# Pieces of one mixer stream placed behind another stream's products in a hybrid trunk kernel

## The chip, the cores and the metric

The kernel runs on one core of a Trainium2 chip. The metric is the time of one execution on the device in microseconds (us). The engines that the text names are TensorE (PE: matrix products and transposes by a product with the identity; PEld is its weight load), VectorE (DVE), ScalarE (ACT), GpSimd (POOL) and SyncE (SP), whose queue issues most of the DMA transfers. Each engine executes its own instructions in program order and waits for the others by semaphores.

## The reference

One layer of a hybrid trunk is applied to a prompt of 16 + 2048 frames and to a sample of 64 frames. An input projection feeds three parallel mixers, whose outputs go through an output projection; a SwiGLU FFN follows. All inputs and outputs are float32.

```python
def _mixer(h, ...):
    proj = h @ w_in                              # 1024 -> 5384
    z, xbc, dt_raw, rw_in, hg_in = _split(proj)  # SSD, RWKV-7, HGRN2 columns
    # Mamba-2 SSD, 8 heads, state 64 x 128
    h = h * exp(cum[-1]) + (xg * exp(cum[-1] - cum)) @ Bm
    y = (L * (Cm @ Bm)) @ xg + (Cm @ h) * exp(cum)
    # RWKV-7, 8 heads, state 64 x 64
    S = S * w + (S @ a) b + v k ;  o = S @ r
    # HGRN2, 4 heads, state 128 x 128
    A = sum(dec * q * k) ;  o = A @ v + (q * exp(cum)) @ S
    S = S * exp(cum[-1]) + (k * exp(cum[-1] - cum)) @ v
    return concat(y_ssd, y_rw, y_hg) @ w_out
x = x + _mixer(rmsnorm(x)) ;  x = x + swiglu(rmsnorm(x)) ;  return rmsnorm(x)
```

Each mixer carries a state from one group of frames to the next, so the tiles of a mixer have to be worked through one after the other.

## The kernel before, in words

**Tiles and stages.** The frames lie in 17 tiles (0 to 16) of up to 128 frames; a chunk has two or three tiles, and there are six chunks (0 to 5), two to a projection block. Weights and activations are split in a high and a low part, and a product is made of three matmuls (high by high, high by low, low by high). The stages are

1. the projection of three blocks (`projection()`), which writes its results to DRAM, where the mixers fetch them tile by tile;
2. the early FFNs for tiles 0 to 8 (`early()`): output projection (`out`), SwiGLU column groups (`ffn`), and the last of its second projection (`rest`). The last of these FFNs stops after 18 column groups (`SWITCH = 18`);
3. `drain(ALLY(range(NT)))` (L1423): every mixer tile has to be done here. Then the `ya` tiles of the late stage are loaded from what the mixers stored (L1434, 24 DMAs on SP), and the last early FFN goes on (`ffn(SWITCH, NFF)`, `rest()`);
4. the late stage for tiles 9 to 16, whose first products have the names `g<-w,op`; `op` is made from `ya` (L1416, L1417).

The matmuls of stages 1, 2 and 4 are called products here; their PSUM banks are named `g` (late also `d`).

**The mixers as streams.** The mixers are Python generators, and a piece is what one yields. RWKV (`rw_mixer`, banks `c` and `po`) is one stream, `rw`. HGRN (`hg_mixer`, L758) and SSD (`ss_mixer`, L886) are woven into one other, `hs` (`hs_mixer`, L979): a step of it runs one piece of HGRN and one of SSD, some 13 steps to a tile. Both write the PSUM bank `h`, of which there is one (L514). HGRN's input tile `hin` also exists once (L761): its last part K is written by L882 and stored by L883 (GpSimd's queue), and the load for the next tile, on SP, waits for that. SSD loads `sin` and `dec` in the same way, one buffer each. `dt`, `cu` and `ex` (L464 and following) are made once for each chunk, in four buffers, and are last used by SSD.

**What sets the order.** Products are generators too, which yield their length in units of 2360 columns (`COL`). `flow` adds it to a clock `now`, and steps every stream whose due time `t` the clock has reached. A step sets t to max(t, now − 1) + d · scale, where d is what the piece yields; for `hs` that is 6.0 × 1.03 = 6.18 units a step. `drain` steps the streams without the clock, until the tiles asked for are done. From the instructions in the order in which they are written down like this, a scheduler sets the final order on each engine by its own model of the times, so that an instruction can move against its neighbours.

The core of it, before:

```python
        def step(self):
            d = next(self.gen, None)
            if d is None:
                self.live = False
            else:
                self.t = max(self.t, now[0] - 1.0) + d * self.scale
    ...
    def flow(gen):
        for cost in gen:
            now[0] += cost
            for s in list(streams):
                while s.live and s.t <= now[0]:
                    s.step()
```

Of the kernel before, what the change touches and what calls it, by code (L numbers as in the profile page):

```python
# [19 lines left out]
P = 128  # L20
# [19 lines left out]
GLO = 3  # L40
URB = 6
RWX, HSX, HSD = 1.08, 1.03, 6.0
COL = 1 / 2360
AHEAD = 4
KOUT = [8, 9, 10, 11, 0, 1, 2, 3, 4, 5, 6, 7]
# [33 lines left out]
def body(tc, A, O, blocks=None, supers=None, dbg=None):  # L79
    nc = tc.nc  # L80
    V, S, G, T = nc.vector, nc.scalar, nc.gpsimd, nc.tensor
# [26 lines left out]

    def mm(out, lhsT, rhs, start, stop, more=False):

        return T.matmul(out, lhsT, rhs, start=start, stop=stop, skip_group_check=more)  # L111

    def in_turn(ins):

# [4 lines left out]
    flat = lambda ap: ap.rearrange("p a b -> p (a b)")  # L119
# [36 lines left out]
    ident = cload("ident", [P, P], p=cst)  # L156
# [91 lines left out]
    def transposed(h, k4, n, hi, lo, col, bank):  # L248

        pt = by(bank(), P)  # L250
        for k in range(4):
            T.transpose(pt[:, k, :n], h[:n, k * P:(k + 1) * P], ident[:n, :n])
        ho, lw = (x[:, 4 * k4:4 * k4 + 4, col:col + n] for x in (hi, lo))
        S.activation(ho, pt[:, :, :n], AF.Copy)
        V.tensor_tensor(lw, pt[:, :, :n], ho.bitcast(F32), SUB)
# [46 lines left out]
    class Chunk:  # L302
        def __init__(self, ci):
            self.ci, self.tiles = ci, CHUNKS[ci]
            self.lens = [LEN[t] for t in self.tiles]
            self.N = sum(self.lens)
            self.nt = len(self.tiles)
            self.offs = [sum(self.lens[:i]) for i in range(self.nt)]
            self.first = self.tiles[0] == 0
# [120 lines left out]
        def dt(self, ps):  # L430

            N, nt = self.N, self.nt
            q0 = 32 * (self.ci % 2)
            st, idq = dst[q0:q0 + 16], ident[q0:q0 + 16, q0:q0 + 16]
            S.activation(st[:, :N], ps[:16, :N], AF.Copy)
            yield
            pt = by(gbank()[:, :48], 16)
            for j in range(nt):
                n, o = self.lens[j], self.offs[j]
                T.transpose(pt[:n, j, :], st[:, o:o + n], idq)  # L440
            sm = lambda tag: mk(gp, [P, 3, 8], tag=tag, bufs=1)[:, :nt]
            dx, ax, u, u2, pl = sm("dx"), sm("ax"), sm("du"), sm("du2"), sm("pl")
            bias = _bc(cb[:, 0:8], 1, nt)
            if self.first:
                G.memset(dx, 0.0)
                V.tensor_tensor(dx[:80, 0, :], pt[:80, 0, 0:8], cb[:80, 0:8], ADD)
                V.tensor_tensor(dx[:, 1:, :], pt[:, 1:nt, 0:8], bias[:, 1:], ADD)
                V.tensor_tensor(dx[:80, 0, :], pt[:80, 0, 8:16], dx[:80, 0, :], ADD)
                V.tensor_tensor(dx[:, 1:, :], pt[:, 1:nt, 8:16], dx[:, 1:, :], ADD)
            else:  # L450
                V.tensor_tensor(dx, pt[:, :nt, 0:8], bias, ADD)
                V.tensor_tensor(dx, pt[:, :nt, 8:16], dx, ADD)
            V.scalar_tensor_tensor(ax, dx, -1.0, dx, MUL, MAX)
            S.activation(ax, ax, AF.Exp, scale=-1.0)
            V.tensor_scalar(u, ax, 2.0, None, ADD)
            V.reciprocal(u, u)
            V.tensor_tensor(u, u, ax, MUL)
            V.tensor_tensor(u2, u, u, MUL)
            V.tensor_scalar(pl, u2, 1.0 / 15.0, None, MUL)
            for k in (13, 11, 9, 7, 5, 3):  # L460
                V.scalar_tensor_tensor(pl, pl, 1.0 / k, u2, ADD, MUL)
            V.scalar_tensor_tensor(pl, pl, 1.0, u, ADD, MUL)
            V.tensor_scalar(dx, dx, 0.0, None, MAX)
            res = mk(dtp, [P, 2, 3, 8], tag="dt", bufs=4)  # L464
            V.scalar_tensor_tensor(res[:, 0, :nt], pl, 2.0, dx, MUL, ADD)
            if self.first:
                V.tensor_scalar(res[:, 0, 0], res[:, 0, 0], c("vmask"), None, MUL)
            la = res[:, 1]
            V.tensor_tensor(la[:, :nt], res[:, 0, :nt], _bc(nea, 1, nt), MUL)

            j0 = 1 if self.first else 0
            yield
            p1 = gbank()[:, 0:72].rearrange("p (a j h) -> p a j h", a=3, h=8)
            mm(flat(p1[:, 0, j0:nt]), triu, flat(la[:, j0:nt]), True, True)
            mm(flat(p1[:, 1, j0:nt]), ones, flat(la[:, j0:nt]), True, True)
            if self.first:
                mm(p1[:, 0, 0], triu0, la[:, 0], True, True)
                mm(p1[:, 1, 0], blk1, la[:, 0], True, True)
                mm(p1[:, 2, 0], ones[0:64, :], la[0:64, 0], True, True)
            cu = mk(dtp, [P, 3, 8], tag="cu", bufs=4)  # L480
            ex = mk(dtp, [P, 3, 3, 8], tag="ex", bufs=4)
            V.tensor_copy(cu[:, :nt], p1[:, 0, :nt])
            V.tensor_copy(ex[:, 0, :nt], p1[:, 0, :nt])
            V.tensor_tensor(ex[:, 1, :nt], p1[:, 1, :nt], cu[:, :nt], SUB)
            V.tensor_copy(ex[:, 2, j0:nt], p1[:, 1, j0:nt])
            if self.first:
                V.tensor_copy(ex[:, 2, 0], p1[:, 2, 0])
            S.activation(ex[:, :, :nt], ex[:, :, :nt], AF.Exp)
            if self.first:
                V.tensor_scalar(ex[:, 0, 0], ex[:, 0, 0], c("smask"), None, MUL)  # L490
            yield
            pt = gbank()
            for j in range(nt):
                T.transpose(pt[:8, j * P:(j + 1) * P], cu[:, j], ident)
            S.activation(st[:8, :nt * P], pt[:8, :nt * P], AF.Copy)
            nc.sync.dma_start(cscr[self.ci].rearrange("j h i -> h j i"), by(st[:8, :nt * P], P))
            self.dtres, self.cu, self.ex = res, cu, ex
# [33 lines left out]
    def rw_mixer(t):  # L531
        ci, j = where[t]
        n = LEN[t]
# [5 lines left out]
        rv, kv, vt = rin[:, 0:4], rin[:, 4:8], rin[:, 8:12]  # L539
# [45 lines left out]
        BK = b4k().rearrange("p (a b c) -> p a b c", b=2, c=64)  # L585
# [6 lines left out]
        for p2 in range(2):  # L592
            pb = cbank(), cbank()
            ins = []
# [29 lines left out]
        for q in range(2):  # L624
            pb = cbank()
            for i in range(4):
                T.transpose(pb[:, i * P:(i + 1) * P], flat(BK[:, 4 * q + i]), ident)
            S.activation(tbk[:, 4 * q:4 * q + 4, :], by(pb, P), AF.Copy)
            yield 1.0
        Z = b4k().rearrange("p (c h q) -> p c h q", c=2, q=64)  # L630
        G.memset(Z[0:64], 0.0)
        pv = cbank()
        for p in range(4):
            T.transpose(pv[:, p * P:(p + 1) * P], vt[:, p], ident)
        for cc in range(2):
            S.activation(flat(Z[64:128, cc]), pv[64 * cc:64 * cc + 64, :], AF.Copy)
        for q in range(31):
# [89 lines left out]
    def rw_tail(t, po, sg, bv):  # L727
# [15 lines left out]
        yield 6.0  # L743
        ptr = by(cbank(), P)
        for p in range(4):
            T.transpose(ptr[:, p, :], of[:, p * P:(p + 1) * P], ident)
        pg = by(cbank(), P)
        for p in range(4):
            mm(pg[:, p, :], g2[:, p * P:(p + 1) * P], sg, True, True)
# [8 lines left out]
    def hg_mixer(t):  # L758
# [81 lines left out]
        yield  # L840
        pk = hbank()
        for h in range(4):
            T.transpose(pk[:, h * P:(h + 1) * P], K[:, h, :], ident)
        Kt = F
        S.activation(flat(Kt), pk, AF.Copy)
        if t == 0:
# [30 lines left out]
        yield  # L877
        pt = by(hbank(), P)
        for h in range(4):
            T.transpose(pt[:, h, :], yt[:, h], ident)  # L880
        V.tensor_tensor(gate, gate, b4(hgwh), MUL)
        V.tensor_tensor(K, pt, gate, MUL)  # L882
        G.dma_start(yscr[2][t], K)  # L883
# [2 lines left out]
    def ss_mixer(t):  # L886
# [25 lines left out]
        for g in range(2):  # L912
            mm(pcb[:, g * P:(g + 1) * P], Bm[:, g], Cm[:, g], True, True)
        for g in range(2):
            T.transpose(pcb[:, 256 + g * P:256 + (g + 1) * P], Bm[:, g], ident)
        cB_ = us()
        cbm = by(cB_[:, 0:256], P)
        V.tensor_tensor(cbm, by(pcb[:, 0:256], P), _bc(tri, 1, 2), MUL)
# [5 lines left out]

        px = hbank()
        for q in range(4):
            T.transpose(px[:, q * P:(q + 1) * P], x[:, q], ident)
        xdt = flat(x)
        V.tensor_tensor(h64(xdt), h64(px), _bc(dt, 2, 64), MUL)
        yb = us()  # L930
# [39 lines left out]
        yield  # L970
        pt = by(hbank(), P)
        for q in range(4):
            T.transpose(pt[:, q, :], yb[:, q * P:(q + 1) * P], ident)
        ys = M2[1]
        V.tensor_tensor(ys, pt, b4(c("ssdw")), MUL)
        G.dma_start(yscr[0][t], ys)
# [11 lines left out]
    now = [0.0]  # L988

    class Stream:  # L990
        def __init__(self, gen, scale):
            self.gen, self.scale, self.t, self.live = gen, scale, now[0], True

        def step(self):
            d = next(self.gen, None)
            if d is None:
                self.live = False
            else:
                self.t = max(self.t, now[0] - 1.0) + d * self.scale

    def mixers(kind, fn):
        for t in range(last_tile + 1):
            while t not in ready[kind]:
                yield 0.5
            yield from fn(t)
# [12 lines left out]
    def flow(gen):  # L1018

        for cost in gen:  # L1020
            now[0] += cost
            for s in list(streams):
                while s.live and s.t <= now[0]:
                    s.step()
            streams[:] = [s for s in streams if s.live]

    def drain(keys):
# [84 lines left out]
                nc.sync.dma_start(O["p_shift"], carry)  # L1112
                nc.sync.dma_start(O["p_conv"], ccarry)

    streams += [Stream(mixers("rw", rw_mixer), RWX), Stream(mixers("hs", hs_mixer), HSX)]
    flow(projection())
    stG.close()

# [165 lines left out]
    if supers:  # L1284
# [192 lines left out]
        def turned(h, j, k4):  # L1477
            pt = by(ybank(), P)
            for k in range(4):
                T.transpose(pt[:, k, :], hs[h, j][k4][:, k * P:(k + 1) * P], ident)  # L1480
            return pt

        hop = {}
# [296 lines left out]
```

## Time and profile before

| | |
|---|---|
| time, median of 3 runs | 3547.19 us (3545.42 to 3551.86) |
| time of the profiled execution | 3539.1 us |
| its span in the profile | 3537.3 us |
| mean granted clock of TensorE | 0.982 |
| TensorE busy | 3367.3 us, 95% |
| VectorE busy | 2216.0 us, 63% |
| ScalarE busy | 1227.5 us, 35% |
| GpSimd busy | 745.9 us, 21% |
| moved by DMA | 860.41 MB, 243 GB/s |

The profile is of one execution. A row of a timeline has the start in us, the duration in us, the engine, the line, the operation, `out<-in` by the names of the tiles, shapes, and a count of like instructions in a row; in brackets stands how long the engine idled ahead of it, and what it waited for. A row of windows has, for a stretch of the span, its length and the busy time of PE, PEld, DVE, ACT and POOL (instructions in parentheses), then the granted clock of TensorE (1 is full speed), the busy share of the DMA engines and GB/s. A row of a tile has the least, median and greatest duration in ns, and the first and last start. The chain rows follow back, from the last instruction, what each step waited for. In the matmul rows the line is mostly that of the helper `mm` (L111, L112 after the change), so the names of the tiles tell what a row is.

### The profile page before, as it was taken

To read this page: it belongs to the slowest core of one execution; us is meant where nothing else is said; L and a number is where in the kernel's file an instruction comes from. 1 tells how busy PE (TensorE), PEld (TensorE's weight loads), DVE (VectorE), ACT (ScalarE), POOL (GpSimd) and SP (SyncE) were. 2 spreads that over 40 slices of the span, in tenths; PEclk is the share of its full clock that TensorE was granted. 3 is DMA by queue.
4 is the path that set the end of the run, shared out by engine and by line. 5 is a ranking of instruction groups with operands and counts; after the bars stand their busy time and mean duration, and the time that the engine had idled before them with its cause. 6 is when DMAs were issued, how large, how long until landed. Compare 5 with 4: busy or idle time off the path is not lost.

```text
span 3537.3 us, 61018 instructions
## 1 busy us (share of the span) xinstructions
PE 3367.3 (95%) x22588; PEld 2940.6 (83%) x22588; DVE 2216.0 (63%) x4961; ACT 1227.5 (35%) x2635; POOL 745.9 (21%) x1058
## 2 busy tenths in 40 slices
PE   7999999999999998889898999999989989999999
PEld 7999789899799996778786899879988868778887
DVE  3358556568666677687876767666524666555553
ACT  4445333244333444344342222222111352223342
POOL 3324202102112112444442120110101003320101
PEclk9999999999999998999999999999999999999999
DMA  9776875565775668888889898686688548775866
GB/s 323 232 229 212 296 228 166 162 174 171 247 225 172 193 198 266 290 308 302 298 312 329 308 325 269 208 286 220 222 278 261 185 141 284 272 264 170 289 202 214
DMA packets 431218, 860.41 MB, mean 243 GB/s; under 512 B 112432, under 2 KB 212280, under 8 KB 428872
## 3 DMA queue, kind: packets, MB, share of 16 engines
q1 hardware_dynamic: 403592, 765.79, 66.1%
q0 software_dynamic: 27328, 90.72, 6.9%
q8 instruction: 178, 2.92, 0.3%
q14 instruction: 120, 0.98, 0.1%
HBM read 603.81 MB, written 252.54 MB: 242 GB/s over the span
## 4 chain that ended last, share of the span: by engine, by line
PE 64%; DMA 13%; DVE 11%; issue 6%; POOL 2%; ACT 2%; SPq 2%; POOLq 0%; DVEq 0%; ACTq 0%
PE g L111 46%; PE d L111 8%; PE c L111 4%; PE h L111 3%; DMA w<-w 3%; DMA raw<-in_w_down 2%; DVE tp L640 1%; DVE Xp L641 1%; DMA hin<-hg 1%; DMA raw<-in_w_up 1%; POOL w L222 1%; DMA hg<-stage 1%; DVE gcv L418 1%; DMA dec<-cu 1%; DVE acc L1278 0%
## 5 line engine op out<-in xcount | busy, mean ns | idle before, releaser
L111 PE MATMUL g<-hhi,w 128*128 128x384 f32 (+3 forms) x3312 | 832.0, 330 | 10.3 <-DMA w<-w 4.1
L111 PEld LDWEIGHTS g<-hhi,w 128*128 128x128 f32 (+1 forms) x3312 | 579.9, 188 | 24.3 <-POOL w L222 4.3
L111 PE MATMUL g<-h2hi,w 128*128 128x384 f32 (+1 forms) x2112 | 549.5, 336 | 19.5 <-DMA w<-w 6.7
L111 PE MATMUL g<-hlo,w 128*128 128x384 f32 (+3 forms) x1680 | 551.2, 328 | 0.0
L111 PEld LDWEIGHTS g<-h2hi,w 128*128 128x128 f32 x2112 | 376.6, 190 | 33.4 <-ACT w L220 7.7
L111 PE MATMUL g<-h2lo,w 128*128 128x384 f32 (+1 forms) x1056 | 349.9, 332 | 0.0
L111 PEld LDWEIGHTS g<-hlo,w 128*128 128x128 f32 (+1 forms) x1680 | 313.9, 187 | 6.8 <-issue 0.9
L222 POOL TENSOR_TENSOR w<-raw,w 128x512 fp32r<-128x512 f32 x180 | 246.7, 1373 | 343.8 <-ACT w L220 273.0
L111 PE MATMUL g<-w,mhi 128*128 128x512 f32 x792 | 259.2, 403 | 12.0 <-DMA w<-w 4.0
L220 ACT ACTIVATE w<-raw 128x512 fp32r<-128x512 f32 x240 | 150.3, 629 | 207.9 <-PE g L111 58.3
L111 PEld LDWEIGHTS g<-h2lo,w 128*128 128x128 f32 x1056 | 200.4, 190 | 2.9
L111 PE MATMUL g<-w,op 128*128 128x512 f32 x816 | 194.4, 397 | 3.1 <-ACT op L1416 3.1
L111 PEld LDWEIGHTS g<-w,op 128*128 128x128 f32 x816 | 153.4, 189 | 41.6 <-ACT op L1416 3.5
L111 PEld LDWEIGHTS g<-w,mhi 128*128 128x128 f32 x792 | 144.5, 188 | 48.3 <-DVE acc L1278 7.6
L111 PE MATMUL g<-w,hhi 128*128 128x512 f32 (+1 forms) x544 | 176.3, 404 | 7.4 <-DMA w<-w 4.3
L111 PE MATMUL d<-op,w 128*128 128x512 f32 x720 | 168.8, 392 | 2.8 <-DVE w L1356 2.8
L111 PEld LDWEIGHTS d<-op,w 128*128 128x128 f32 x720 | 135.0, 188 | 33.5 <-DVE w L1356 4.1
L1278 DVE TENSOR_TENSOR acc<-g,acc 128x512 f32<-128x512 f32 (+1 forms) x198 | 132.1, 682 | 44.0 <-PE g L111 43.9
L640 DVE TENSOR_TENSOR tp<-Xp,b4k 128x60 f32<-128x60 f32 (+24 forms) x527 | 126.8, 241 | 51.2 <-DMA b4k<-psc 38.3
L111 PE MATMUL g<-w,mlo 128*128 128x512 f32 x396 | 155.6, 393 | 0.0
L111 PE MATMUL d<-w,op 128*128 128x512 f32 x612 | 143.9, 395 | 0.0
L111 PEld LDWEIGHTS d<-w,op 128*128 128x128 f32 x612 | 114.7, 187 | 28.1
(437 smaller groups left out, 6233.0 us busy)
## 6 DMA issues: line engine op xcount, KB each, us to landing
w<-w SPq DMA_DIRECT2D x893, 512.0 KB, 4.4
hin<-hg SPq DMA_DIRECT2D x16, 1280.0 KB, 8.4
rin<-rw SPq DMA_DIRECT2D x16, 896.0 KB, 7.1
raw<-in_w_gate SPq DMA_DIRECT2D x56, 256.0 KB, 4.5
raw<-in_w_up SPq DMA_DIRECT2D x56, 256.0 KB, 4.5
hg<-stage SPq DMA_DIRECT2D x64, 192.0 KB, 2.5
raw<-in_w_out SPq DMA_DIRECT2D x48, 256.0 KB, 4.6
sin<-ss SPq DMA_DIRECT2D x16, 768.0 KB, 4.9
```

Of the source, the lines that this page charges most:

```text
L111: return T.matmul(out, lhsT, rhs, start=start, stop=stop, skip_group_check=more)
L220: S.activation(hi, raw, AF.Copy)
L222: (G if units[0] % 4 < GLO else V).tensor_tensor(lo, raw, wt[:, 0], SUB)
L418: V.scalar_tensor_tensor(cvt[:, :M], raw[:, j:j + M], tap(j), cvt[:, :M], MUL, ADD)
L640: V.tensor_tensor(tv, _bc(Xp[:, 0:m, q], 2, w), _bc(Up[:, q, q + 1:32], 1, m), MUL)
L641: V.tensor_tensor(Xp[:, 0:m, q + 1:32], Xp[:, 0:m, q + 1:32], tv, ADD)
L1278: V.tensor_tensor(self.acc[:n, i, cs], ps[:n], self.acc[:n, i, cs], ADD)
```

## The change

The stream `hs` gets a number `late` = 4.0 (`LATE_`); `rw` has 0. In `flow` a stream is stepped by itself when t + late has been reached by the clock. When a step of a stream without `late` has issued at least one TensorE instruction, `ride` steps the stream `hs` once, if its t is at most now + 4; the first TensorE instruction of that step gets a dependency without a semaphore on the last one of the step before, so that the scheduler can't put it ahead. For this the helpers `mm` and `turn` (which stands where `T.transpose` stood) remember the last TensorE instruction. `drain` steps as before. The rule by which a step sets t is the same as before.

```diff
+LATE_ = 4.0
...
-        return T.matmul(out, lhsT, rhs, start=start, stop=stop, skip_group_check=more)
+        return noted(T.matmul(out, lhsT, rhs, start=start, stop=stop, skip_group_check=more))
+
+    def turn(out, x, idn):
+        return noted(T.transpose(out, x, idn))
+
+    pe = [None, None]
+
+    def noted(ins):
+        if pe[1] is not None:
+            tc.add_manual_dep(ins.ins, pe[1].ins.name, mybir.DependencyInfo(
+                mybir.DependencyClass.NoSync, mybir.DependencyReason.DATA), reason="behind")
+            pe[1] = None
+        pe[0] = ins
+        return ins
...
     class Stream:
-        def __init__(self, gen, scale):
-            self.gen, self.scale, self.t, self.live = gen, scale, now[0], True
+        def __init__(self, gen, scale, late=0.0):
+            self.gen, self.scale, self.late, self.t, self.live = gen, scale, late, now[0], True
 
         def step(self):
+            before = pe[0]
             d = next(self.gen, None)
             if d is None:
                 self.live = False
             else:
                 self.t = max(self.t, now[0] - 1.0) + d * self.scale
+            return pe[0] is not before
+
+    def ride():
+
+        for s in streams:
+            if s.late and s.live and s.t <= now[0] + s.late:
+                pe[1] = pe[0]
+                s.step()
+                pe[1] = None
...
-                while s.live and s.t <= now[0]:
-                    s.step()
+                while s.live and s.t + s.late <= now[0]:
+                    if s.step() and not s.late:
+                        ride()
...
-    streams += [Stream(mixers("rw", rw_mixer), RWX), Stream(mixers("hs", hs_mixer), HSX)]
+    streams += [Stream(mixers("rw", rw_mixer), RWX), Stream(mixers("hs", hs_mixer), HSX, LATE_)]
```

The instructions are the same before and after; their order differs. Three places show how.

**First place: TensorE in the third projection block.** `c` is RWKV, `h` is HGRN or SSD, `g` are products. Before:

```order
L111 MATMUL g_14752<-hhi_10693,w_14812 128x256
L111 MATMUL c_14706<-TT,ur_14558 32x32
L111 MATMUL g_14752<-hhi_10693,w_14812 128x256
L111 MATMUL c_14706<-TT,ur_14558 32x32 x15
L111 MATMUL c_14767<-Srw_13238,rin_13379 64x64 x8
L111 MATMUL c_14767<-b4k_14031,L_13854 64x64 x8
L111 MATMUL g_14752<-hlo_10694,w_14812 128x256
```

Now, at a like place:

```order
L112 MATMUL g_14868<-w_14973,hlo_10049 128x512
L112 MATMUL c_14510<-TT,ur_14350 32x32 x16
L112 MATMUL c_14571<-Srw_13080,rin_13219 64x64 x8
L112 MATMUL c_14571<-b4k_13895,L_13679 64x64 x8
L112 MATMUL h_14593<-us_14483,onesr 128x512
L112 MATMUL h_14593<-us_14484,onesr 128x512
L112 MATMUL g_14869<-w_14973,hhi_10048 128x512 x2
```

A piece of HGRN stands right behind RWKV's, where a product stood behind RWKV's. Over the whole program the groups of mixer pieces between two products go from 602 to 491.

**Second place: TensorE at the dt matmuls of the same block** (`g<-dt,triu` and `g<-dt,onesr`, made once for a chunk; the chunks here are 4 and 5). Before:

```order
L111 MATMUL g_13327<-hlo_10694,w_13381 128x256
L111 MATMUL g_13327<-hhi_10693,w_13381 128x256
L111 MATMUL g_13469<-dt_12926,triu 128x24
L111 MATMUL g_13469<-dt_12926,onesr 128x24
L111 MATMUL g_13479<-dt_12954,triu 128x16
L111 MATMUL g_13479<-dt_12954,onesr 128x16
L111 MATMUL g_13489<-hhi_10150,w_13491 128x384
```

Now:

```order
L112 MATMUL g_13293<-dt_12733,onesr 128x24
L115 MATMUL h_12478<-ident,hin_10926 128x128 x4
L112 MATMUL h_12786<-sin_12590 128x128 x2
L115 MATMUL h_12786<-ident,sin_12590 128x128 x2
...
L112 MATMUL h_12876<-us_12781,onesr 128x512
L112 MATMUL h_12876<-us_12782,onesr 128x512
...
L115 MATMUL h_12881<-ident,sin_12590 128x128 x4
L112 MATMUL c_12959<-b4k_12294,L_12109 64x64 x8
L112 MATMUL h_12927<-sin_12590,dec_12592 64x64 x16
L112 MATMUL c_12993<-ur_12978,TT 64x64 x4
L112 MATMUL g_13303<-dt_12761,triu 128x16
L112 MATMUL g_13303<-dt_12761,onesr 128x16
```

Between the dt matmuls of the two chunks stand now the end of HGRN's tile 4 (its transpose, `h_12478`), the first SSD pieces and the first HGRN sums of tile 5, with pieces of RWKV, and no product.

**Third place: the end of the mixers.** On TensorE before, the last piece (the transpose ahead of K, L880) stands among products of the early FFN (`mhi`, `mlo`: its second projection):

```order
L111 MATMUL g_28302<-w_28298,mhi_27871 128x512 x2
L111 MATMUL g_28302<-w_28298,mlo_27872 128x512
L880 MATMUL h_28255<-ident,hin_27407 128x128 x4
L111 MATMUL g_28302<-w_28300,mhi_27871 128x512 x2
L111 MATMUL g_28302<-w_28300,mlo_27872 128x512
```

Now the early FFN's last product is followed by 158 matmuls of `h`, tiles 15 (from `h_28347`) and 16 (`hin_28497`), up to the first product of the late stage:

```order
L112 MATMUL g_29213<-w_29143,mlo_28950 128x512
L112 MATMUL h_28347<-Sss,sin_28272 128x256 x2
L112 MATMUL h_28358<-us_28314,us_28296 128x256 x2
L112 MATMUL h_28363<-us_28353,onesr 128x512
L112 MATMUL h_28363<-us_28354,onesr 128x512
L112 MATMUL h_28387<-hin_28270 128x128 x4
L115 MATMUL h_28397<-ident,us_28312 128x128 x4
...
L112 MATMUL h_28706<-hin_28497 128x128 x4
L115 MATMUL h_28718<-ident,hin_28497 128x128 x4
L112 MATMUL g_29262<-w_29269,op_29266 128x512 x2
```

On SP's queue the loads `ya` lay among the weight loads before:

```order
L216 DMA w_28371<-w_19054 128x1024
L216 DMA w_28386<-w_19074 128x1024
L1434 DMA ya_28736<-y_9_199 128x4x128
L1434 DMA ya_28736<-y_10_200 128x4x128
L1434 DMA ya_28736<-y_11_201 128x4x128
L1434 DMA ya_28736<-y_12_202 128x4x128
L1434 DMA ya_28736<-y_13_203 128x4x128
L1434 DMA ya_28736<-y_14_204 128x4x128
L216 DMA w_28400<-w_19111 128x1024
```

and lie now behind all weight loads of the early FFN and five of the late stage, and behind the three loads of tile 16:

```order
L230 DMA w_29314<-w_15508 128x1024
L230 DMA w_29331<-w_15564 128x1024
L910 DMA sin_28499<-ss_149 128x1536
L919 DMA dec_28501<-cu_155 128x1024
L784 DMA hin_28497<-hg_143 128x2560
L1459 DMA ya_28736<-y_9_199 128x4x128
L1459 DMA ya_28736<-y_10_200 128x4x128
```

More of the change, by code (lines that the diff above doesn't have):

```diff
@@ L251, in transposed @@
         for k in range(4):
-            T.transpose(pt[:, k, :n], h[:n, k * P:(k + 1) * P], ident[:n, :n])
+            turn(pt[:, k, :n], h[:n, k * P:(k + 1) * P], ident[:n, :n])
         ho, lw = (x[:, 4 * k4:4 * k4 + 4, col:col + n] for x in (hi, lo))
@@ L439, in dt @@
                 n, o = self.lens[j], self.offs[j]
-                T.transpose(pt[:n, j, :], st[:, o:o + n], idq)
+                turn(pt[:n, j, :], st[:, o:o + n], idq)
             sm = lambda tag: mk(gp, [P, 3, 8], tag=tag, bufs=1)[:, :nt]
@@ L493, in dt @@
             for j in range(nt):
-                T.transpose(pt[:8, j * P:(j + 1) * P], cu[:, j], ident)
+                turn(pt[:8, j * P:(j + 1) * P], cu[:, j], ident)
             S.activation(st[:8, :nt * P], pt[:8, :nt * P], AF.Copy)
@@ L626, in rw_mixer @@
             for i in range(4):
-                T.transpose(pb[:, i * P:(i + 1) * P], flat(BK[:, 4 * q + i]), ident)
+                turn(pb[:, i * P:(i + 1) * P], flat(BK[:, 4 * q + i]), ident)
             S.activation(tbk[:, 4 * q:4 * q + 4, :], by(pb, P), AF.Copy)
@@ L633, in rw_mixer @@
         for p in range(4):
-            T.transpose(pv[:, p * P:(p + 1) * P], vt[:, p], ident)
+            turn(pv[:, p * P:(p + 1) * P], vt[:, p], ident)
         for cc in range(2):
@@ L745, in rw_tail @@
         for p in range(4):
-            T.transpose(ptr[:, p, :], of[:, p * P:(p + 1) * P], ident)
+            turn(ptr[:, p, :], of[:, p * P:(p + 1) * P], ident)
         pg = by(cbank(), P)
@@ L842, in hg_mixer @@
         for h in range(4):
-            T.transpose(pk[:, h * P:(h + 1) * P], K[:, h, :], ident)
+            turn(pk[:, h * P:(h + 1) * P], K[:, h, :], ident)
         Kt = F
@@ L879, in hg_mixer @@
         for h in range(4):
-            T.transpose(pt[:, h, :], yt[:, h], ident)
+            turn(pt[:, h, :], yt[:, h], ident)
         V.tensor_tensor(gate, gate, b4(hgwh), MUL)
@@ L914, in ss_mixer @@
         for g in range(2):
-            T.transpose(pcb[:, 256 + g * P:256 + (g + 1) * P], Bm[:, g], ident)
+            turn(pcb[:, 256 + g * P:256 + (g + 1) * P], Bm[:, g], ident)
         cB_ = us()
@@ L926, in ss_mixer @@
         for q in range(4):
-            T.transpose(px[:, q * P:(q + 1) * P], x[:, q], ident)
+            turn(px[:, q * P:(q + 1) * P], x[:, q], ident)
         xdt = flat(x)
@@ L972, in ss_mixer @@
         for q in range(4):
-            T.transpose(pt[:, q, :], yb[:, q * P:(q + 1) * P], ident)
+            turn(pt[:, q, :], yb[:, q * P:(q + 1) * P], ident)
         ys = M2[1]
@@ L1479, in turned @@
             for k in range(4):
-                T.transpose(pt[:, k, :], hs[h, j][k4][:, k * P:(k + 1) * P], ident)
+                turn(pt[:, k, :], hs[h, j][k4][:, k * P:(k + 1) * P], ident)
             return pt
```

## The prediction

> **What bounds the kernel now.** I began with the page: its span, its first part (busy time by engine), its fourth (the chain of work that ended last) and one row of its sixth (DMA issues).
>
> ```profile
> span 3537.3 us, 61018 instructions
> PE 3367.3 (95%) x22588; PEld 2940.6 (83%) x22588; DVE 2216.0 (63%) x4961; ACT 1227.5 (35%) x2635; POOL 745.9 (21%) x1058
> ...
> PE 64%; DMA 13%; DVE 11%; issue 6%; POOL 2%; ACT 2%; SPq 2%; POOLq 0%; DVEq 0%; ACTq 0%
> ```
>
> TensorE is busy for 95% of the span, so an edit gains only by taking time out of TensorE's own stream or out of the 170 us in which it stands still, and it loses wherever TensorE's next instruction in program order is not ready. The same matrix products have to be done either way. The question is therefore where the new order leaves TensorE with mixer pieces and no product to put between them. I then went to the timeline of TensorE, for what it costs to switch between products (bank `g`) and pieces of RWKV (`c`) or of HGRN and SSD (`h`), and to places where it has nothing but pieces.
>
> **Part 1: the merges.** By the order, 602 islands of mixer pieces between products become 491, 111 fewer, while the instructions stay the same; islands of RWKV and HGRN/SSD pieces without a third kind rise from 34 to 78. Three places in the timeline of TensorE now (start, duration, then the group; matmuls overlap, so I take start to start) price one merge: an RWKV piece alone, an HGRN/SSD piece alone, and both together.
>
> ```profile
> 737.83 0.34 PE L111 MATMUL g<-hlo,w 128*128 128x384 f32 x1
> 738.10 1.16 PE L111 MATMUL c<-rin,b4k 64*128 64x128 f32 x14
> 739.18 0.62 PE L111 MATMUL g<-hhi,w 128*128 128x384 f32 x2
> ...
> 728.97 0.34 PE L111 MATMUL g<-hlo,w 128*128 128x384 f32 x1
> 729.14 1.02 PE L111 MATMUL h<-Sss,sin 128*128 128x256 f32 x4
> 729.82 0.69 PE L111 MATMUL g<-hhi,w 128*128 128x384 f32 x2
> ...
> 605.03 0.34 PE L111 MATMUL g<-hlo,w 128*128 128x384 f32 x1
> 605.29 1.16 PE L111 MATMUL c<-rin,b4k 64*128 64x128 f32 x14
> 606.38 1.13 PE L111 MATMUL h<-Sss,sin 128*128 128x256 f32 x4
> 607.16 0.70 PE L111 MATMUL g<-hhi,w 128*128 128x384 f32 x2
> ```
>
> From product to product RWKV alone takes 739.18 − 737.83 = 1.35 us, HGRN/SSD alone 0.85, together 607.16 − 605.03 = 2.13. Both alone contain one product's own issue time, 0.17 to 0.18 us (728.97 to 729.14), which is counted once too often in their sum: 1.35 + 0.85 − 0.17 = 2.03. So this merge costs 0.10 us. A second pair goes the other way:
>
> ```profile
> 705.28 0.34 PE L111 MATMUL g<-hhi,w 128*128 128x384 f32 x1
> 705.46 0.63 PE L111 MATMUL h<-us,onesr 128*128 128x512 f32 x2
> 705.92 0.33 PE L111 MATMUL g<-hhi,w 128*128 128x384 f32 x1
> ...
> 598.88 0.34 PE L111 MATMUL g<-hhi,w 128*128 128x384 f32 x1
> 600.23 0.50 PE L111 MATMUL h<-us,onesr 128*128 128x256 f32 x2
> 600.57 0.33 PE L111 MATMUL g<-hhi,w 128*128 128x384 f32 x1
> ```
>
> Alone 0.64 us, so 1.35 + 0.64 − 0.17 = 1.82 for the two; together (14 RWKV matmuls stand between the first two rows of the second group) 600.57 − 598.88 = 1.69, a gain of 0.13, and of that 0.13 is what the narrower tile (0.50 against 0.63) explains. Bounds for 111 merges: −14 to +11 us. I take 0, the middle, and what the second pair says when its width is allowed for.
>
> [...]
>
> **Part 2: the pace.** Behind the new test a lone step of HGRN and SSD runs when the clock stands at or above its due time plus 4. Its next due time is the larger of its own and the clock less 1, plus 6.18 (6.0 × 1.03). A lone step therefore starts from t + 4 − 1, three units later than before, and the stream, when it has to walk alone, steps each 9.18 units instead of each 6.18. Rides cost no such delay, but need RWKV to issue TensorE work inside the window. So HGRN and SSD fall behind. The order shows it: before, the last `h` matmul stands at product 10215 of the early part, afterwards behind the last one, 10812. In the drain that separates the last early FFN's first 18 column groups from the rest, 28 steps of HGRN and SSD are left where there was none. These are tile 15 from its HGRN masks on and the whole of tile 16: 30 pieces, 158 matmuls, which stand on TensorE one behind another with no product in between, because the scheduler has put every remaining product of the early FFN ahead of them.
>
> What does such a bare chain cost? The kernel now has one stretch in which TensorE has nothing but mixer pieces, between the projection's last product and the first one of the early FFNs; its windows row gives busy time, granted clock (0.61) and DMA share, and the timeline its HGRN/SSD pieces:
>
> ```profile
> 1356.00:1380.00 24.00, 14.13 (x103) 10.23 (x102) 20.29 (x43) 12.18 (x27) 5.40 (x5) 0.61 0.82 282
> ...
> 1359.52 0.70 PE L111 MATMUL h<-us,onesr 128*128 128x512 f32 x2 [2.65 <-ACT Pt L560]
> 1362.93 2.05 PE L111 MATMUL h<-hin 128*128 128x128 f32 x8 [1.81 <-DVE At L816]
> 1367.69 1.12 PE L973 MATMUL h<-ident,us 128*128 128x128 f32 x4 [2.71 <-DVE At L822]
> 1370.01 2.07 PE L111 MATMUL h<-hin 128*128 128x128 f32 x8 [1.20 <-DVE dec L975]
> 1373.41 0.41 PE L111 MATMUL h<-hin 128*16 128x16 f32 x32 [0.42 <-DVE hin L832]
> 1376.07 0.64 PE L111 MATMUL h<-hin 128*32 128x32 f32 x16
> 1378.64 1.11 PE L111 MATMUL h<-hin 128*64 128x64 f32 x8
> ```
>
> Seven pieces with six intervals in 1378.64 − 1359.52 = 19.1 us: 3.2 us a piece, and VectorE is busy for 20.3 of these 24 us, since RWKV runs on it as well. In the tail RWKV is done, so 3.2 is the upper bound. Lower bound: the shortest intervals of these rows (1370.01 − 1367.69 = 2.3, 1378.64 − 1376.07 = 2.6) less half of the matmul group in them for full clock (0.5 of 1.12, 0.5 of 0.64): 1.7 and 2.3, about 2.0. I take 2.5: 30 × 2.5 = 75 us (60 to 96).
>
> Between tile 15 and tile 16 lies a transfer that nothing covers. HGRN's input buffer `hin` is single; the load of the next tile waits until the store of K has left:
>
> ```profile
> hin<-hg SPq DMA_DIRECT2D x16, 1280.0 KB, 8.4
> ...
> 2485.46 0.69 DVE L882 TENSOR_TENSOR hin<-h,hin 128x512 f32<-128x512 f32 x1
> 2498.39 0.69 DVE L783 TENSOR_TENSOR At<-hin 128x512 f32<-128x512 f32 x1 [3.75 <-DMA hin<-hg]
> 2597.88 0.69 DVE L882 TENSOR_TENSOR hin<-h,hin 128x512 f32<-128x512 f32 x1 [0.57 <-PE h L880]
> ```
>
> From the end of K at 2486.15 to the first operation on the new tile 12.2 us pass, 8.4 of them the load. Today products stand over it. SSD's tile 16 may fill some of it on TensorE; its pieces are counted among the 30 all the same. Tail: 75 + 12.2 = 87.2 us. From that goes the TensorE time that these pieces take now among products: 0.85 and 0.64 us from product to product above, less the product's 0.17, so about 0.6 each: 30 × 0.6 = −18.
>
> **Part 3: the restart behind the tail.** The loads `ya` of the late stage (24 on SP's queue) read what the mixers stored, and the last rows of K are stored at the end of the tail. They go out among the weight loads now; rows of the tile `ya` and the windows there:
>
> ```profile
> L1434 SPq DMA_DIRECT2D ya<-y x24: 518/634/1887, 2601.8 to 2630.3; - x24
> L1416 ACT ACTIVATE op<-ya x21: 1041/1048/1063, 2728.4 to 2826.8; 128x1024 fp32r<-128x1024 f32 x21
> L1417 DVE TENSOR_TENSOR op<-ya,op x21: 1214/1225/1256, 2731.4 to 2827.9; 128x1024 fp32r<-128x1024 f32 x21
> ...
> DMA to landing us min/median/max: 5.2/7.4/8.7
> ...
> 2595.00:2640.00 45.00, 35.48 (x168) 30.44 (x168) 11.18 (x18) 2.56 (x5) 0.55 (x1) 0.96 1.05 322
> ...
> 2729.46 4.83 PE L111 MATMUL g<-w,op 128*128 128x512 f32 x12 [3.11 <-ACT op L1416]
> ```
>
> In 2595 to 2640 TensorE lacks 45.00 − 35.48 = 9.5 us, with the DMA engines full (share 1.05): the `ya` loads hold up weights there. In the new order on SP all but five weights are issued ahead of `ya`, so this loss goes: −9.5. In exchange the late stage starts from cold: K's end to the first `ya` issue 2601.8 − 2598.6 = 3.2; three more issues at (2630.3 − 2601.8) / 23 = 1.24, 3.7; landing 5.2, the least seen, since nothing else moves; the copy 1.05 and the subtraction 1.23: 14.4, less the 3.1 that TensorE idles ahead of that product today: +11.3. What waits behind it on SP is the rest of `ya`, and TensorE with it.
>
> [...]
>
> **Part 4: a stall in the third projection block.** `dt`, `cu` and `ex` have four buffers, one per chunk, freed by the last SSD use. In the new order chunk 5's two dt matmuls (second order piece for TensorE above) stand behind tile 5's first SSD pieces, and these behind the end of tile 4, K, the load of `hin` and the first sums, with not one product in the 90 matmuls of that island. Cost: the same 12.2 us, plus some nine short operations at about 0.7 (the rows of 0.69 above), 6, less about 6 us of TensorE work in the island, which is done anyway: +12; bounds 0 (if HGRN and SSD have already got so far) and 18.
>
> **Sum**, against the profiled execution: its own time 3539.1 (1.8 above its span), + 87.2 tail − 18 − 9.5 + 11.3 + 12 + 0 merges = 3622.1 us. The median of the runs shown, 3547.19, lies 8.1 above that execution, so 3630 us, a ratio of 1.023. By the lower ends (tail 72, dt 0, merges −14) it is 3589, by the upper (tail 108, dt 18, merges +11) 3668.
>
> **Rivals.**
> *A, the other side: not slower.* If an exit from the 64-row tiles costs more than these two pairs show, say the 0.10 us by which RWKV's entry is longer (0.27 against 0.17), on both sides, 111 merges give 0.2 each, 22 us. To decide, the tail would have to be cheap as well: with −18 − 9.5 + 11.3, no dt stall and −22 it comes to zero at 38 us for the tail, 0.9 us a piece beside the load. At 0.6 a piece, bare TensorE time, the time is 3547 − 38 + 30 = 3539. Against it: no interval among the rows above is under 2.3 us, and every piece but a few has an operation of VectorE or ScalarE between itself and the next. That the change does nothing is ruled out by the order.
>
> *B, the tail goes at today's pace.* The tail of tile 16 runs now at the pace of its stream; the rows of the chain there:
>
> ```profile
> 2559.95 0.45 PE h L111 x4
> ...
> 2597.41 0.44 PE h L880 x4
> ```
>
> Seven intervals in 37.5 us, 5.35 a piece. If that were the chain of operations itself and not the planner, the tail would be 30 × 5.35 + 12.2 = 173 us and the time 3715. Against it: between these pieces lie 23 to 29 products of TensorE each, its own work, and the free stretch had 3.2.
>
> *C, a shorter tail.* HGRN and SSD pieces of one step overlap on the other engines: 20 steps at 2.0 instead of 30 pieces, 40 + 12.2 = 52 us, no dt stall: 3583.
>
> **How the numbers follow.** Forecast 0.80, A 0.07, B 0.05, C 0.08. The likeliest gives 3630. Range: from C's time to the upper sum, 3583 to 3668, which leaves out A, B and some of C, under 2 in 10. This kernel's runs tell 0.2%, 7 us, from no change. Faster by more than that is half of A, 0.04; within it the other half, 0.03; slower the rest, 0.93.
>
> **What would show it.** In the profile afterwards: a stretch of some 70 to 110 us near 2700 with `h` matmuls, no `g`, TensorE mostly idle and a low granted clock; in its middle a `hin` load of about 8 us with nothing over it; `ya` issued only behind its end; a second stretch without products near 1200 us, at the dt matmuls; switches as dear as before, and the late stage as long as before. Wrong would be: products among the last `h` pieces, a tail under 50 us, or a TensorE sum that falls by 20 us outside the tail.

## The result and the profile after

The changed kernel takes 3670.63 us (median of 4 runs, 3664.86 to 3676.22) where the kernel before takes 3549.53 us (median of 4, 3545.42 to 3552.54): a ratio of 1.0336, 95% interval 1.0317 to 1.0355. That is slower, as forecast, but by 121 us where 83 were forecast, and 2.6 us above the upper end of the range. The profiled execution of the change took 3670.2 us, almost its median, while that of before lay 10 us under the median given here; from profile to profile the loss is 131 us.

The page of the changed kernel: span, busy time by engine, the granted clock in 40 slices, and the chain that ended last.

```profile
span 3668.4 us, 60989 instructions
...
PE 3398.0 (93%) x22588; PEld 2962.1 (81%) x22588; DVE 2214.0 (60%) x4961; ACT 1231.6 (34%) x2638; POOL 738.0 (20%) x1058
...
PEclk9999999999999899899999999999995999999999
...
PE 54%; DMA 16%; DVE 13%; issue 9%; POOL 3%; SPq 3%; ACT 2%; POOLq 0%; DVEq 0%; ACTq 0%
```

TensorE's part of the chain falls from 64% to 54%; DMA, "issue" and VectorE take its place, and one slice near 2800 us has the clock at 0.5. TensorE's time outside its busy time rises from 3537.3 − 3367.3 = 170 us to 3668.4 − 3398.0 = 270. Two stretches hold 81 us of these 270 (102.00 − 47.23 and 39.00 − 12.80 in the windows rows below). The first is the end of the mixers; rows of the timelines of TensorE, VectorE and SP, and the windows row of the stretch:

```profile
2752.88 0.40 PE L112 MATMUL g<-w,mlo 128*128 128x512 f32 x1
2753.16 1.13 PE L112 MATMUL h<-Sss,sin 128*128 128x256 f32 x4
...
2788.18 0.69 DVE L896 TENSOR_TENSOR hin<-h,hin 128x512 f32<-128x512 f32 x1 [3.29 <-PE h L115]
2791.62 0.32 SPq L784 DMA_DIRECT2D hin<-hg  x1
2797.32 0.69 DVE L797 TENSOR_TENSOR At<-hin 128x512 f32<-128x512 f32 x1 [8.46 <-DMA hin<-hg]
...
2844.09 0.69 DVE L896 TENSOR_TENSOR hin<-h,hin 128x512 f32<-128x512 f32 x1 [1.66 <-PE h L115]
2847.50 19.92 SPq L1459 DMA_DIRECT2D ya<-y  x24
2855.20 7.22 PE L112 MATMUL g<-w,op 128*128 128x512 f32 x24 [11.15 <-ACT op L1441]
...
2753.00:2855.00 102.00, 47.23 (x284) 35.03 (x282) 43.24 (x98) 18.30 (x58) 21.61 (x31) 0.53 0.40 139
```

For 102 us, from 2753.2 to 2855.2, TensorE has no product. It is busy for 47 us of them, at a granted clock of 0.53. (The 158 matmuls of the order are nearly all of the x284: the profile counts some as two, `h<-sin,dec` as 32 where the order has 16.) Tile 15's K is done at 2788.9, the load of `hin` for tile 16 holds VectorE's first operation on it until 2797.3, the last K is done at 2844.8, and only then do the `ya` loads leave. From one K to the next a whole tile of HGRN and SSD by itself takes 2844.8 − 2788.9 = 55.9 us.

The second stretch is at the dt matmuls in the third projection block. In the kernel before TensorE is busy throughout at this place:

```profile
1190.00:1215.00 25.00, 25.00 (x255) 23.61 (x254) 17.29 (x56) 11.12 (x25) 2.78 (x2) 1.00 0.70 208
```

In the changed kernel (TensorE, then VectorE and SP, and the window):

```profile
1218.21 1.06 PE L112 MATMUL c<-ur,L 32*32 32x32 f32 x32 [22.42 <-DVE ur L669]
1219.20 1.22 PE L112 MATMUL h<-us,onesr 128*128 128x512 f32 x2
1227.42 0.37 PE L112 MATMUL g<-dt,onesr 128*128 128x16 f32 x2
...
1201.42 0.18 DVE L654 TENSOR_TENSOR tp<-Xp,b4k 128x24 f32<-128x24 f32 x1
1203.50 0.69 DVE L797 TENSOR_TENSOR At<-hin 128x512 f32<-128x512 f32 x1 [1.90 <-DMA hin<-hg]
1205.04 1.26 DVE L655 TENSOR_TENSOR Xp<-Xp,tp 128x24 f32<-128x24 f32 x1
1209.18 0.17 DVE L655 TENSOR_TENSOR Xp<-Xp,tp 128x8 f32<-128x8 f32 x1
1217.45 0.70 DVE L669 STREAM_TRANSPOSE ur<-ur 32x512 f32<-32x512 f32 x1 [7.80 <-DMA ur<-psx]
...
1209.38 2.55 SPq L661 DMA_DIRECT2D psx<-Xp  x4
1213.34 1.82 SPq L665 DMA_DIRECT2D TT<-psx  x4
...
1189.00:1228.00 39.00, 12.80 (x172) 10.37 (x171) 22.86 (x80) 9.27 (x21) 4.25 (x5) 0.56 0.32 97
```

The reader should look at who stands first. On TensorE it is RWKV's `c<-ur,L`, ahead of HGRN's sums `h<-us,onesr`, and it waits for 22.4 us. It waits for RWKV's solve (`tp`, `Xp`), whose result takes a way through DRAM (`psx`): out at 1209.4, back for VectorE at 1217.5. And the solve is late: its last five steps stand on VectorE behind HGRN's first operation on the new `hin` (1203.50), which waits for the load, and then alternate with operations of HGRN and SSD until 1209.3. In the run `slow` below the same five steps take 1.0 us (1175.56 to 1176.57). So some 6 to 7 us of TensorE's wait are this hold (an estimate: from 1201.6 to 1209.35, less 1.0), and 8.1 are the way through DRAM.

With the products counted through on both timelines, the shift between the two kernels at the same product tells where the time went:

| from, to | shift at the end | added |
|---|---|---|
| start, product 5000 (before: 1180 us) | −4.5 us | −4.5 |
| product 5100, behind the dt matmuls | +31.7 | +36.2 |
| product 10790, near the end of the early FFN | +26.7 | −5.0 |
| product 10812, the first of the late stage | +125.7 | +99.1 |
| last product | +130.7 | +5.0 |

### The profile page after: what moved, and what is told of

Same layout as the page of the kernel before. It is cut to its first block, busy times and chain, and to the rows that moved or that the text cites. A ratio compares the mean times of both kernels' runs of the same rounds, so it can differ in the third digit from the quotient of the medians.

```text
span 3668.4 us, 60989 instructions
## 1 busy us (share of the span) xinstructions
PE 3398.0 (93%) x22588; PEld 2962.1 (81%) x22588; DVE 2214.0 (60%) x4961; ACT 1231.6 (34%) x2638; POOL 738.0 (20%) x1058
## 4 chain that ended last, share of the span: by engine, by line
PE 54%; DMA 16%; DVE 13%; issue 9%; POOL 3%; SPq 3%; ACT 2%; POOLq 0%; DVEq 0%; ACTq 0%
PE g L112 38%; PE d L112 7%; PE c L112 4%; PE h L112 3%; DMA w<-w 3%; DMA raw<-in_w_down 2%; DMA hin<-hg 2%; DVE tp L654 1%; DVE Xp L655 1%; DMA b4k<-psc 1%; DVE gcv L432 1%; POOL w L236 1%; DMA raw<-in_w_up 1%; DMA y<-hin 1%; PE po L112 1%
## 5 line engine op out<-in xcount | busy, mean ns | idle before, releaser
L112 PE MATMUL g<-hhi,w 128*128 128x384 f32 (+3 forms) x3312 | 821.6, 328 | 12.4 <-DMA w<-w 5.4
L112 PE MATMUL g<-w,op 128*128 128x512 f32 x816 | 194.9, 397 | 12.6 <-ACT op L1441 12.6
```

Of the source, the lines that this page charges most:

```text
L112: return noted(T.matmul(out, lhsT, rhs, start=start, stop=stop, skip_group_check=more))
```

## The experiments

Two things come with the change: islands that are merged by an ordered ride, and HGRN and SSD that lag. The first four runs separate them. **The pace given back**, with rides as they are:

```diff
-                self.t = max(self.t, now[0] - 1.0) + d * self.scale
+                self.t = max(self.t, now[0] - 1.0 - self.late) + d * self.scale
```

> The change with one line altered: a step of the stream with `late` sets t to max(t, now - 1 - late) + d * scale, so a lone step no longer sets the stream three units back. Riding stays: 502 islands of mixer pieces by the order (before 602, the change 491), last h matmul at product 10575 of 10812, no island without products above 70 matmuls. Theory lag (the loss comes from HGRN and SSD falling behind, merges are worth about nothing): 3535 to 3560 us, no stretch without products over 30 us. Rival merges pay 0.2 us each: about 3530 us. Rival merges cost (each ride holds up TensorE): above 3570 us.

Measured: 3586.27 us, 1.0079 (1.0065 to 1.0092) times before. With 100 islands fewer than before the tail is gone and so is the dt stretch; three quarters of the loss go with the pace. It stays 0.8% slower. Of the three expectations the time meets the last one, that each ride holds up TensorE (above 3570 us), and its busy TensorE time isn't lower than before's either. The largest single wait of the rest stands at the end of the early FFN (SP, VectorE and TensorE):

```profile
2705.44 0.69 DVE L896 TENSOR_TENSOR hin<-h,hin 128x512 f32<-128x512 f32 x1 [1.34 <-PE h L115]
2709.11 20.02 SPq L1459 DMA_DIRECT2D ya<-y  x24
2729.24 2.91 SPq L230 DMA_DIRECT2D w<-w  x5
2734.98 1.22 PE L112 MATMUL g<-w,mhi 128*128 128x512 f32 x2 [17.65 <-DMA w<-w]
```

The last K is done 108 us later than in the kernel before. Now all 24 `ya` issues run through SP in one piece of 20 us, with weights behind them, and TensorE waits 17.7 us for a weight, where the `ya` loads cost it 9.5 us before. So this wait explains some 8 of the 29 us of loss; what the dependency has to do with the rest is taken up below.

**The lag without a ride**: the kernel before with its stream slowed.

```diff
-RWX, HSX, HSD = 1.08, 1.03, 6.0
+RWX, HSX, HSD = 1.08, 1.24, 6.0
```

> The kernel before (no late, no riding) with HSX 1.24 in place of 1.03, so that HGRN and SSD step each 7.44 units in place of 6.18. By the order 600 islands, as before, but 178 h matmuls behind the last early product and 78 matmuls between the two dt pairs. Theory lag: the loss of the change without any riding: a stretch of 95 to 120 us without products near 2700 us and one of 20 to 40 us near 1200 us, 3640 to 3690 us. Rival riding causes the loss: 3550 to 3580 us.

Measured: 3630.18 us, 1.0206 (1.0187 to 1.0224). No ride, as many islands as before, and the tail of the change stands there: TensorE, VectorE and SP around it, and around its dt matmuls.

```profile
2804.36 0.69 DVE L882 TENSOR_TENSOR hin<-h,hin 128x512 f32<-128x512 f32 x1 [3.93 <-PE h L880]
2815.99 2.50 PE L111 MATMUL g<-w,op 128*128 128x512 f32 x5 [11.67 <-ACT op L1416]
...
2706.00:2816.00 110.00, 48.94 (x319) 36.00 (x317) 47.04 (x107) 19.94 (x61) 22.77 (x32) 0.54 0.36 131
...
1176.60 2.55 SPq L647 DMA_DIRECT2D psx<-Xp  x4
1180.63 0.38 PE L111 MATMUL g<-dt,onesr 128*128 128x24 f32 x2
1196.07 0.61 PE L111 MATMUL g<-dt,triu 128*128 128x16 f32 x2
```

110 us without products at the end, as expected, and 15 at the dt matmuls (1180.6 to 1196.1), where 20 to 40 were expected. The time is under the expected 3640, in part because of that. Here RWKV's solve goes out to DRAM before the stretch begins (`psx` at 1176.6) and is back on VectorE at 1186.9: its matmuls lie in the island too, but TensorE waits there for operations of HGRN and SSD alone (3.4, 0.8 and 2.3 us).

**The dt stretch taken out**: five buffers for dt, cu and ex.

```diff
-            res = mk(dtp, [P, 2, 3, 8], tag="dt", bufs=4)
+            res = mk(dtp, [P, 1, 3, 8], tag="dt", bufs=5)
-            la = res[:, 1]
+            la = mk(gp, [P, 3, 8], tag="la", bufs=2)
-            cu = mk(dtp, [P, 3, 8], tag="cu", bufs=4)
-            ex = mk(dtp, [P, 3, 3, 8], tag="ex", bufs=4)
+            cu = mk(dtp, [P, 3, 8], tag="cu", bufs=5)
+            ex = mk(dtp, [P, 3, 3, 8], tag="ex", bufs=5)
```

> The change with five buffers in place of four for dt, cu and ex (the second half of dt goes to a tile of its own), so that chunk 5's dt needn't wait for tile 5's SSD. By the order no dt island any more, a tail of 192 h matmuls in place of 160. Theory: the 38 us stretch at 1200 us goes, the tail grows by 32 matmuls, some 5 pieces at 2.5 us: 3670 - 38 + 13 = 3645 us (3630 to 3660). Rival, the stall only moves to the next place where HGRN and SSD are due: 3670 us.

Measured: 3667.24 us, 1.0308 (1.0287 to 1.0329), hardly less than the change. The stretch is gone (at product 10790, near the end of the early FFN, this kernel is some 42 us ahead of the change), and the tail is longer (K's operations on VectorE, the first late product, the window):

```profile
2714.00 0.69 DVE L896 TENSOR_TENSOR hin<-h,hin 128x512 f32<-128x512 f32 x1
2778.97 0.69 DVE L896 TENSOR_TENSOR hin<-h,hin 128x512 f32<-128x512 f32 x1 [2.42 <-PE h L115]
2836.03 0.69 DVE L896 TENSOR_TENSOR hin<-h,hin 128x512 f32<-128x512 f32 x1 [3.93 <-PE h L115]
2847.07 3.35 PE L112 MATMUL g<-w,op 128*128 128x512 f32 x7 [11.07 <-ACT op L1441]
...
2712.00:2847.00 135.00, 52.97 (x328) 38.41 (x328) 54.70 (x121) 20.41 (x60) 23.06 (x33) 0.54 0.32 114
```

Two whole tiles with two loads of `hin` are in it, 135 us instead of 102. The rival was nearer: most of the gain moved, 33 of the 42 us into the tail. The likely reason, argued from the two traces and not tried alone, is that a stall in which TensorE waits for HGRN and SSD is also time in which these catch up; without it they arrive at the end with more left.

**The dependency taken out** of the change, so that the scheduler may place a ride where it likes; one execution (`nodep`), then four (`nodep2`):

```diff
-                pe[1] = pe[0]
+                pe[1] = None
```

> The change without the dependency that holds a ride behind RWKV's instruction; pace and rides as in the change. By the order 581 islands, a tail of 150 h matmuls, no dt island, an island of 121 matmuls at the end of the projection. Theory lag: a tail of about 95 us without products as in the change, 3630 to 3660 us. Rival, the dependency itself is what costs: under 3580 us.

> The kernel of the run nodep again, timed in rounds: the change without the dependency alone. The one look gave 3615 us where the change has 3667 to 3671 us. Theory in-order wait: the difference is 25 us of waits and the dt stretch of 38 us that the dependency makes, less its other island: 1.3 to 1.8% slower than before. Rival, the one look was a stray: 3% slower.

Measured: 3614.88 us in the one execution, which is between the two expectations; then 3619.3 us, 1.0191 (1.0169 to 1.0214), just above what was expected for `nodep2`. The tail is there again, the dt stretch is not:

```profile
2697.00:2796.00 99.00, 39.42 (x267) 29.49 (x265) 36.36 (x82) 17.06 (x52) 19.16 (x29) 0.55 0.39 137
```

Ahead of its tail, by products, this kernel is 30 us ahead of the kernel before. Over products 5000 to 5100, where the change loses 36.2 us, it gains 5.3. So the lag by itself makes the tail, and at the dt matmuls at most the short stretch of `slow`; the long one comes only where lag and dependency meet. How the dependency leads the scheduler to that order was not followed.

The next four ask for the price of a ride where nothing lags: the run `pace` without the dependency, and HSX 0.95 with rides and dependency (`pace95`), with rides alone (`p95n`), and without rides (`b95`).

> The kernel of the run pace (rides, a lone step keeps its pace) without the dependency that holds a ride behind RWKV's instruction. By the order 576 islands of mixer pieces (pace 502), last h matmul at product 10035 (pace 10575, before 10215). Theory in-order wait (a ride that is held behind RWKV's last instruction makes TensorE wait where the scheduler would have put a product first): the idle time of TensorE inside islands falls back by some 20 us against pace, and the ya loads come early again (another 18): within 0.4% of before. Theory late end only (pace lost only by its ya loads, which hold up weights): the same time here, but pace95 is then within 0.4% as well.

> The kernel of the run pace with HSX 0.95 in place of 1.03: merges as in pace (517 islands by the order), the last h matmul at product 10024 in place of 10575, so no lag at the end and the ya loads early. Theory in-order wait: still 0.4 to 0.7% slower than before, with TensorE's idle time ahead of product 10000 some 20 us longer. Theory late end only: within 0.3% of before. Rival A of the prediction (each merge pays 0.2 us): 0.5% faster.

> The kernel before with HSX 0.95 in place of 1.03 and nothing else: HGRN and SSD earlier, no riding (570 islands by the order). Both theories: within 0.4% of before; it is the same pace as pace95 without rides, so that pace95 less this run is what riding costs or brings: in-order wait +15 to +25 us, late end only 0, rival A -15 us.

> The kernel of the run pace95 (HSX 0.95) without the dependency: 575 islands by the order, last h matmul at product 9500. With b95 (no rides, +0.5%) and pace95 (rides with the dependency, +0.4%) it tells what the dependency costs where nothing lags. Theory in-order wait: 0.4 to 0.7% faster than pace95, so at before's time or up to 0.2% faster. Rival, HSX 0.95 itself costs (mixer pieces too early, whatever the rides): +0.4% like the other two.

Two more tried neighbours of `pace_nodep`: LATE_ 2.0, and the same kernel once more.

> The kernel of the run pace_nodep with LATE_ 2.0 in place of 4.0 (594 islands by the order, last h matmul at product 10069). Tried as a version that may beat both kernels. Both theories: within 0.3% of before; merges are worth nothing, so no more than pace_nodep's -0.15%.

> The kernel of the run pace_nodep once more, on whatever chip this falls: is its -0.15% (interval -0.28 to -0.03) there again? If it is a gain: -0.05 to -0.3%. If it was chance: an interval that holds zero in its middle.

| run | rides, dependency | HSX | islands by the order | busy TensorE, us | ratio to before (95%) |
|---|---|---|---|---|---|
| before | no, no | 1.03 | 602 | 3367.3 | 1 |
| `pace` | yes, yes | 1.03 | 502 | 3380.8 | 1.0079 (1.0065 to 1.0092) |
| `pace_nodep` | yes, no | 1.03 | 576 | 3375.4 | 0.9985 (0.9972 to 0.9997) |
| `pn_again`, the same | yes, no | 1.03 | 576 | 3380.1 | 0.9974 (0.9959 to 0.9990) |
| `pn2`, LATE_ 2.0 | yes, no | 1.03 | 594 | 3395.1 | 1.0076 (1.0053 to 1.0100) |
| `b95` | no, no | 0.95 | 570 | 3379.1 | 1.0053 (1.0033 to 1.0073) |
| `pace95` | yes, yes | 0.95 | 517 | 3387.7 | 1.0038 (1.0022 to 1.0055) |
| `p95n` | yes, no | 0.95 | 575 | 3383.1 | 1.0072 (1.0051 to 1.0092) |

None of these has a tail. The theory of an in-order wait says that the dependency by itself costs TensorE some 20 us. At HSX 1.03 the runs go its way: `pace` is 0.9% slower than `pace_nodep`, and in the profiled executions TensorE stands still for 3591.7 − 3380.8 = 211 us against 3538.0 − 3375.4 = 163. At HSX 0.95 they don't: `pace95`, with the dependency, is not slower than `p95n` without it, nor than `b95` without rides. So it isn't a price that each ride pays. HSX 0.95 costs 0.5% without rides and 0.9% in the pair with rides alone, but the pair with the dependency is 0.4% faster with it (`pace`, `pace95`). `b95`, `p95n` and `pn2` came out slower than every one of their expectations. Nor does the number of islands order the rows: 502 to 602 islands, and busy TensorE time within 0.9%, never under that of before. All that is left is that a different interleaving moves this kernel by −0.3 to +0.8%; what decides it is not settled, nor why `pn2` and `pace_nodep`, which differ in one number, lie 0.9% apart. `pace_nodep` is under before in both measurements, on two chips, by 0.15 and 0.26%, about the bound of what can be told: the one version here that beats both kernels.

The last run tests the price of the tail by its length: LATE_ 1.0 in the change.

> The change with LATE_ 1.0 in place of 4.0: a lone step comes at t + 1 and is no longer set back three units, but still loses what the clock has overshot. By the order 509 islands, no dt island, and a tail of 90 h matmuls, 16 pieces, without a load of hin in it (the change 30 pieces with one load). Theory lag, sizes from the change's trace (91.6 us for 30 pieces and one load of 8.4, so 2.8 us a piece, then 10.4 to the first product): a stretch without products of 16 x 2.8 + 10 = 55 us (45 to 62), and 1.2 to 2.0% slower than before. Rival, the tail has a fixed cost whatever its pieces: 90 to 100 us without products.

Measured: 3618.51 us, 1.0180 (1.0157 to 1.0204). TensorE's first bare piece, VectorE's last K, and the first late product:

```profile
2734.72 0.73 PE L112 MATMUL h<-us,onesr 128*128 128x512 f32 x2
...
2782.81 0.69 DVE L896 TENSOR_TENSOR hin<-h,hin 128x512 f32<-128x512 f32 x1 [1.67 <-PE h L115]
2794.53 13.54 PE L112 MATMUL g<-w,op 128*128 128x512 f32 x48 [11.76 <-ACT op L1441]
```

2794.5 − 2734.7 = 59.8 us where 55 were expected: 48.8 to K's end, 3.0 us a piece for 16, and 11.0 from there to the product. The tail costs by the piece, with a fixed 10 to 11 us behind it.

## Why the prediction was right or wrong, point by point

**The tail (+87.2) and the restart (14.4, less 3.1): right in mechanism, and lucky in the last digits.** To K's end 91.6 us, which with the load of 8.5 (12.2 taken) leaves 2.8 us a piece (2.5 taken, bounds 2.0 and 3.2); from K's end to the product 10.4. Together 102.0 us measured, 101.6 in the sum, and the shift there is 99.1 against 98.5. That the sums agree so well is luck, as three sizes were off and cancel: the pieces took 8 us more, the load 4 less, the restart 4 less. (The first late product starts right behind the copy, which ends at 2855.15; the subtraction of 1.23 us is not on its path.) Lengths on both sides (`late1`, `dt5`) and a kernel without rides (`slow`) bear it out. Rival B (173 us) and C (52 us) fall; the pace among products was the planner's.

**The merges (0): right in size, and no run here shows a gain from them.** Rival A, whose 0.27 and 0.17 us are 738.10 − 737.83 and 729.14 − 728.97 in the rows of Part 1, falls: where the lag is taken away and 100 merges stay (`pace`), the time is 29 us over before's, and riding at HSX 0.95 (`pace95` against `b95`, 53 merges) moves it by 0.15%, within the intervals. A price well below 0.2 us a merge would be hidden under these shifts.

**The dt stall (+12, bounds 0 to 18): the step that failed.** It was sized as "the same 12.2 us, plus some nine short operations at about 0.7" less 6, a chain of HGRN and SSD alone. Waits for that chain alone are what `slow` has, 15 us from dt to dt. In the change a second chain lies in the same island: RWKV's `c<-ur,L` is first in TensorE's order, its solve is held on VectorE behind the wait for `hin`, and its result goes through DRAM, so that TensorE stands still for 22.4 us at this one place. +36.2 instead of +12. The 90 matmuls of the island were counted, `c` among them, but not what the `c` matmuls wait for. Without the dependency (`nodep2`) and with a fifth buffer (`dt5`) the stretch is gone.

**What the tail gives back (−18 of TensorE work, −9.5 of weights held up): it came, and other waits ate it, to which the sum gave nothing.** The shift outside the two stretches and the late stage is −4.5 − 5.0 = −9.5, not −27.5. The `ya` stall did go: the 9.5 us that TensorE lost between products 10250 and 10811 are 0.4 in the change. But outside its two stretches TensorE stands still in the change for 270.4 − 54.8 − 26.2 = 189 us, against 170 before with the `ya` stall still in it. Outside their tails it is 3607.4 − 3392.8 − 59.6 = 155 us in `nodep2`, which differs by the dependency alone, and 3658.3 − 3408.6 − 82.0 = 168 in `dt5`, which has it. At product 10790 `nodep2` is 29.9 us ahead of before, `slow` 20.4, `dt5` 15.9. So in the change these waits go with the dependency, some 34 us of them; they are spread over many places, and how it makes each of them was not followed.

**The late stage (no change): +5.0.** Its first `op` tiles follow `ya` loads that are issued over 20 us, but TensorE's wait for `op` is 12.6 us in the whole page of the change, 11.15 of it the restart, so that this explains 1.4 us; the rest is open.

In sum 98.5 + 12 − 27.5 = 83 was forecast; 99.1 + 36.2 − 9.5 + 5.0, 130.7 before rounding, was found: 24 of the missing 48 us are the dt stall, 18 what the tail gives back, 5 the late stage. The range was too narrow by its own terms: its upper end let the tail, the dt stall and the merges reach their bounds, but the dt bound of 18 held one chain where there were two, and the −27.5 had no bounds at all.

## What to carry to other kernels

When a change makes one stream wait longer before it may run, look first at the rate that follows from the rule, and at where the backlog has to be paid: here a lone step cost 9.18 units in place of 6.18, and the bill came at the barrier that asks for all tiles, at about 3 us a piece and a whole load in the open. Where a stall is priced, go through every stream that has instructions in that island, on each engine's own order, and not only the one that the stall is named after. And a stall that is removed in the middle can return at the end while the stream is as late as before: in `dt5` 33 of 42 us did.

## What the runs showed of the hardware

In the bare chains at the end of the mixers the granted clock was 0.53 in the change (with TensorE busy for 47 of 102 us), 0.52 in `late1`, 0.54 in `slow` and `dt5` and 0.55 in `nodep2`. It was 0.56 in the dt stretch of the change; in that of `slow`, 15 us long, it was 0.69. The group of four `h<-Sss,sin` took 1.02 us among products in the kernel before (at 729.14), and 1.13 as the first group of the change's chain (2753.16) and 2.08 in its middle (2811.46); what the low clock costs the chain as a whole was not measured. If all of TensorE's time shrank with the clock, it would be 47.2 × (1 − 0.53) = 22 of the 102 us, an estimate from above. The other 55 us are waits: by what ended them 22.8 for VectorE, 11.2 for the first copy into `op` behind the `ya` loads, 11.1 for an operation of ScalarE behind the one load of `hin`, 7.3 for ScalarE elsewhere, and 2.9 with no wait that the profile shows. The load of `hin` for tile 16 took 5.7 us from its issue to the first use (2791.6 to 2797.3, at 230 GB/s, which is its 1280 KB and nothing else), against a median of 8.4 from issue to landing in the kernel before, where the loads go among those of weights, so that the open transfer cost less than the covered ones suggested.
